# Rebuilding the tail of an encoder layer: the embedding product moved into the last attention units, all tokens through seven-product passes 384 columns wide, weight splits placed later

## The chip, the cores and the metric

The kernel runs on one core of a Trainium2 chip. The metric is device time in microseconds of one execution. Three runs of the kernel before took 2616.91, 2618.83 and 2621.61 us; the median is 2618.83. The engines are called by their short names: PE (TensorE), DVE (VectorE), ACT (ScalarE), POOL (GpSimd) and SP (SyncE, which issues the transfers).

## The reference

Two sequences (a prompt and a sample) of 2048 tokens, model width 1024, share one set of weights; all is float32.

```python
def encoder_layer(x, p, norm_w, w_in, ..., w_out, w_ple, w_ple_gate):
    h = rms_norm(x, norm_w)
    q_a, k_a, v_a, g_a, q_b, k_b, v_b, g_b = jnp.split(h @ w_in, IN_SPLITS, axis=-1)
    ...
    o_a = windowed_gqa_sink(q_a, k_a, v_a, sink_a) * jax.nn.silu(g_a)
    ...
    o_b = neighbourhood_attn(q_b, k_b, v_b, rpb_b) * jax.nn.silu(g_b)
    x = x + jnp.concatenate([o_a, o_b], axis=-1) @ w_out
    gate = jax.nn.sigmoid(x @ w_ple_gate)
    return x + (p @ w_ple) * gate
```

Branch A is attention in a window of 128 tokens to each side (8 query heads, 2 key heads, width 64), with QK-norm, a partial rotary embedding and a sink for each head. Branch B is neighbourhood attention over a grid of 64 columns (8 heads) with QK-norm and a position bias. `p` has 256 columns.

## The kernel before

**Float32 by three passes.** Each operand of a matmul is split into a high part (a rounded `fp32r` copy, made by ACT) and a low part (the rest, a subtraction on DVE or POOL), and each product is three matmuls: hi·hi, lo·hi, hi·lo. In the profile a split of a weight shows as ACT L146 and DVE L147 (`split_w`, with the norm's weight as a factor), or L150 and L151 (without).

**Phases.** Phase A goes over 32 tiles of 128 tokens, with two attention units each (`sc` scores, `pt` transposes, `po` output), phase B over 64 units of 128 tokens and 4 heads (`scb`, `ptb`, `pob`). Between an attention unit's steps the program puts matmuls of a *stream* of other work, which a generator gives out step by step: the projections of phase A (`pk`, `pq`, `pg`), then those of phase B (`pqk`, `pvg`, twice, for two halves of the heads), then `out_ahead`. `PLAN_A` and `PLAN_B` say at which share of a unit's budget of PE time which step comes; the last units have a budget of `TAIL`. Each engine works through its own instructions in the order that results from this. SP issues all transfers in one order.

**Weights.** The weights of the stream lie in 16 slots `wa0..7` and `wb0..7`. When a part of the stream ends, `paired` loads the next weights over them with `load_w`, which also puts one job (a split) for each slot into the list `jobs`. Every fourth step of the stream runs one job (`pump`); at the start of a projection `flush("wa")` or `flush("wb")` runs all of that name that are left. `stats_b` (L512), a few small DVE operations that make the norm's factors for a sequence from its sums of squares, is called when a projection has been given out.

**The tail.** The out projection of the first 4 tiles of 256 tokens is done by `out_ahead` (L811) as a plain product over 1024 rows, 192 matmuls of 256 columns each (`pout`), three tiles inside the last attention units and one behind them; the sum with `x` is made by DVE L831 (`ev`) and written to DRAM (`x_d`). The remaining 6 groups of 512 tokens of the out projection (stage 0) and all 8 of the gate (stage 1) go through a scheme of seven products of half-size blocks in place of eight: the weights' sums are prepared in phase A (`sums`), `prep` makes the seven right operands (`opd`, from the raw blocks `oar`, `obr` or `x1r`; sums on DVE and POOL at L993 to L1004, high part ACT L977/L979, low part DVE or POOL L993), `product` (L1014) issues 48 matmuls 256 columns wide for each, into accumulators `acca` and `accc`, and `result` evacuates them: a copy into `r` by ACT (L1059) or a sum with `x` by DVE (L1054), later sums into `r` (L1064), and in stage 1 a tanh on ACT (L1068), the product with the embedding part (DVE L1069) and the sum with `x1` (DVE L1071). The embedding product `pple` (768 matmuls of 256) stands between the products of stage 1. `prep` runs two products ahead of `product`. Accumulators come in the PSUM pools of the phases before (`pj` three buffers, `sc` three, `ms` two).

Of the kernel before, what the change touches and what calls it, by code (L numbers as in the profile page):

```python
# [18 lines left out]
SEQ = 2048  # L19
# [51 lines left out]
TW = 256  # L71
NU = SEQ // TW
AHEAD = 4
# [15 lines left out]
def emit(ctx, tc, io):  # L89
# [3 lines left out]
    pp = ctx.enter_context(tc.tile_pool(name="psum", bufs=2, space=bass.MemoryType.PSUM))  # L93
# [50 lines left out]
    def split_w(w, raw, sc, pin=lambda ins: ins):  # L144
        if sc is not None:
            nc.scalar.activation(w[:, 0], raw, AF.Copy, scale=sc)  # L146
            nc.vector.scalar_tensor_tensor(out=w[:, 1], in0=raw, scalar=sc, in1=w[:, 0].bitcast(F32),  # L147
                                           op0=ALU.mult, op1=ALU.subtract)
        else:
            pin(nc.scalar.copy(w[:, 0], raw))  # L150
            pin(nc.vector.tensor_tensor(out=w[:, 1], in0=raw, in1=w[:, 0].bitcast(F32), op=ALU.subtract))  # L151

    jobs = []
# [9 lines left out]
    def load_w(pool, tag, src, c0, nk, scaled):  # L163

        ws = []
        for j in range(nk):
# [3 lines left out]
            jobs.append((tag, partial(split_w, w, raw, nw[:, j:j + 1] if scaled else None)))  # L170
# [67 lines left out]

    P = tc.keep_in_program_order
# [144 lines left out]
    def proj_a(f):  # L384
# [41 lines left out]
        for i, c in enumerate(project(pq, xr, lambda k, b: w_q[k][:, b, :], 215)):  # L426
# [6 lines left out]
            if i == PD and late:  # L433
                late.pop()()
            yield c
# [36 lines left out]
        if f == NT + 9:  # L472
            stats_b(0)
# [130 lines left out]
    def proj_b(f):  # L604
# [5 lines left out]
        if f == 2 * NT + 9:  # L610
            stats_b(1)
# [4 lines left out]
        flush("wa")  # L616
        pk = ptile([128, 512], "pj", "pqk")
        for i, c in enumerate(project(pk, xr, lambda k, b: w_qk[k][:, b, :], 215)):
            at = i + 24 if f in last else i
            if at in HX:  # L620
                split(f + 1, HX[at])
            yield c
# [15 lines left out]
        flush("wb")  # L638
        pv = ptile([128, 512], "pj", "pvg")
        for i, c in enumerate(project(pv, xr, lambda k, b: w_vg[k][:, b, :], 215)):  # L640
# [117 lines left out]
    tiles = [(s, u) for s in range(2) for u in range(NU)]  # L758
    x1_d = [dram.tile([128, KT, TW], F32, tag=f"x1_d{n}", name=f"x1_d{n}") for n in range(len(tiles))]
    o_st, o_rs = {}, {}  # L760

    def fproj(ps, w, m, xs, nk, mm_):
        for k in range(nk):
            if mm_ is mm:
                flush(f"o{k // 4}")
                flush(("wa", "wb")[m // 4])
            for i, (a, b) in enumerate(((0, 0), (1, 0), (0, 1))):
                mm_(ps, w[m // 4][k][:, a, 128 * (m % 4):128 * (m % 4) + 128], xs(k, b),
                    start=(k == 0 and i == 0), stop=(k == nk - 1 and i == 2))
                yield 108  # L770

    def load_o(n, tail):
        if n < len(tiles):
            s, u = tiles[n]
            o_st[n] = []
            for i in range(2):
                st = main.tile([128, 2, TW], F32, tag="stage", name="oa", bufs=2)
                nc.sync.dma_start(st, oa_d[s].rearrange("(i j p) t -> i p j t", p=128, j=2)[i, :, :, TW * u:TW * u + TW])
                o_st[n].append(st)
            for i in range(2):  # L780
                if tail:
                    st = ap.tile([128, 2, 4, 64], F32, tag="sq", name="ob", bufs=2)
                else:
                    st = main.tile([128, 2, 4, 64], F32, tag="s", name="ob", bufs=SB)
                nc.sync.dma_start(st.rearrange("p j c t -> p (j c) t"),
                                  ob_d[s][u // 2].rearrange("p (i j) c t -> i p (j c) t", i=2)
                                  [i, :, :, 64 * (u % 2):64 * (u % 2) + 64])
                o_st[n].append(st)

    def split_o(n, i):  # L790

        t = main.tile([128, 2, 2, 2, TW], F32R, tag="xr", name="o_r", bufs=2)
        st = o_st[n][2 * i:2 * i + 2]

        def job(dst, src):
            nc.scalar.copy(dst[0], src)
            nc.vector.tensor_tensor(out=dst[1], in0=src, in1=dst[0].bitcast(F32), op=ALU.subtract)
        for j in range(2):
            if i == 0:
                jobs.append((f"o{i}", partial(job, [t[:, j, a] for a in range(2)], st[j])))  # L800
            else:
                for k in range(2):
                    jobs.append((f"o{i}", partial(job, [t[:, j, a, k].rearrange("p (r k c) -> p k r c", k=4, c=16)
                                                        for a in range(2)],
                                                  st[j][:, k].rearrange("p k (r c) -> p k r c", c=16))))
        o_rs.setdefault(n, []).append(t)

    def o_hi_lo(n):
        return lambda k, b: o_rs[n][k // 4][:, k % 4 // 2, b, k % 2, :]

    def out_ahead(n):  # L811

        tail = n < AHEAD - 1
        if n > 0:
            split_o(n, 0)
            split_o(n, 1)
        if n != AHEAD - 2:
            load_o(n + 1, tail)
# [398 lines left out]
```

## Time and profile before

| | |
|---|---|
| median of three runs | 2618.83 us |
| the profiled execution | 2626.2 us |
| its span in the trace | 2624.4 us |
| granted TensorE clock, mean | 0.99 |
| PE, DVE, ACT, POOL busy | 2552.9, 1959.5, 1416.7, 788.5 us |
| instructions of PE | 16080 matmuls |
| moved by DMA | 357.51 MB, mean 136 GB/s |

A row of the timeline or of the chain gives start and length in us, engine, line of the kernel, operation, output <- inputs and shape; `xN` means that N of the same kind stand in one row. In brackets stands how long the engine had been idle and what released it. A line such as L193 is that of the helper that issues all matmuls, so the names of the tiles tell the place. Granted clock 1.00 is full speed.

### The profile page before, as it was taken

The page shows a single profiled execution, that of the slowest core. Times are in us where ns is not written, and L with a number is a line of the kernel's source. Part 1 is how long each engine was busy: PE and PEld are TensorE (multiplying, and loading weights), DVE is VectorE, ACT ScalarE, POOL GpSimd, SP SyncE. Part 2 cuts the span into 40 slices and gives each one's busy share as a digit, 9 for nine tenths or more (in the row PEclk, how much of TensorE's full clock was granted, in tenths as well). Part 3 has the DMA queues.
Part 4 walks back from the last instruction along what each step waited for, and adds up shares of the span by engine and source line. Part 5 has one row for each costly group of instructions (what it writes and reads, how often), then busy time and mean ns, then how long its engine had stood idle before and what let it go on. Part 6 is the DMA issues. An engine that isn't in the chain of part 4 may idle for free.

```text
span 2624.4 us, 46991 instructions
## 1 busy us (share of the span) xinstructions
PE 2552.9 (97%) x16080; PEld 2274.5 (87%) x16080; DVE 1959.5 (75%) x5702; ACT 1416.7 (54%) x3327; POOL 788.5 (30%) x996
## 2 busy tenths in 40 slices
PE   7999999999979999999899999999999999999999
PEld 6888888888867888888788888887999999999999
DVE  6888888888877788888888888888655548555554
ACT  5666666666655566666666666666432214222322
POOL 3332333322323333333233332221122323223321
PEclk9999999999999999999999999999999999999999
DMA  5333322111133555555755555457575446232221
GB/s 176 107 105 105 107 83 93 57 57 59 57 91 118 160 174 170 183 175 157 241 160 162 188 176 152 151 158 214 177 245 183 150 158 208 81 108 97 78 79 47
DMA packets 227520, 357.51 MB, mean 136 GB/s; under 512 B 37937, under 2 KB 115377, under 8 KB 222129
## 3 DMA queue, kind: packets, MB, share of 16 engines
q1 hardware_dynamic: 227280, 354.50, 42.8%
q8 instruction: 128, 2.10, 0.3%
q14 instruction: 112, 0.91, 0.1%
HBM read 266.33 MB, written 105.92 MB: 142 GB/s over the span
## 4 chain that ended last, share of the span: by engine, by line
PE 87%; DVE 6%; DMA 4%; ACT 2%; issue 1%; POOL 0%; SPq 0%; ACTq 0%; DVEq 0%; POOLq 0%
PE pqk L193 13%; PE pvg L193 13%; PE acca L1027 12%; PE accc L1027 9%; PE pg L193 6%; PE pq L193 5%; PE pob L193 4%; PE pple L193 3%; PE scb L193 3%; PE ptb L196 3%; PE sc L193 3%; PE po L193 3%; PE pt L196 3%; PE pk L193 3%; PE pout L193 3%
## 5 line engine op out<-in xcount | busy, mean ns | idle before, releaser
L223 ACT ACTIVATE s<-s,nm 128x384 f32<-128x384 f32 (+4 forms) x512 | 306.4, 600 | 344.3 <-DVE nm L219 185.5
L193 PE MATMUL pvg<-wb,xr 128*128 128x512 f32 x1536 | 458.9, 406 | 0.0
L193 PE MATMUL pqk<-wa,xr 128*128 128x512 f32 x1536 | 436.6, 406 | 0.0
L288 POOL TENSOR_TENSOR xr<-stx,xr 128x512 fp32r<-128x512 f32 x192 | 248.0, 1299 | 205.9 <-ACT xr L287 203.1
L193 PEld LDWEIGHTS pqk<-wa,xr 128*128 128x128 f32 x1536 | 266.8, 189 | 37.2
L193 PEld LDWEIGHTS pvg<-wb,xr 128*128 128x128 f32 x1536 | 270.0, 190 | 32.1
L193 PE MATMUL pg<-wb,xr 128*128 128x512 f32 x768 | 233.0, 411 | 4.3 <-DVE q L445 4.3
L193 PE MATMUL pq<-wa,xr 128*128 128x512 f32 x768 | 223.3, 404 | 3.3 <-ACT wa L146 3.3
L234 POOL TENSOR_TENSOR g<-qg,rd 128x256 f32<-128x256 f32 x64 | 39.4, 615 | 494.0 <-DVE rd L232 480.1
L1027 PE MATMUL acca<-opd,s 128*128 128x256 f32 x1344 | 164.3, 283 | 2.5 <-ACT r L1059 2.5
L193 PEld LDWEIGHTS pq<-wa,xr 128*128 128x128 f32 x768 | 141.5, 192 | 28.1 <-ACT wa L146 3.7
L1027 PEld LDWEIGHTS acca<-opd,s 128*128 128x128 f32 x1344 | 162.6, 192 | 2.9 <-ACT r L1059 2.7
L208 DVE CUSTOM_DVE_ANT_0 s<-scb,bias 128x288 f32<-128x288 f32 (+3 forms) x256 | 141.9, 555 | 28.8 <-PE scb L193 24.5
L193 PEld LDWEIGHTS pg<-wb,xr 128*128 128x128 f32 x768 | 138.6, 191 | 25.2 <-issue 4.6
L721 ACT CAST p_t<-ptb 96x384 fp32r<-96x384 f32 (+3 forms) x256 | 130.0, 509 | 50.1 <-PE ptb L196 48.5
L722 DVE TENSOR_TENSOR p_t<-ptb,p_t 96x384 fp32r<-96x384 f32 (+3 forms) x256 | 149.0, 584 | 9.0 <-ACT p_t L721 6.3
L600 ACT ACTIVATE ks_b<-pktb,wk 64x128 fp32r<-64x128 f32 x256 | 125.5, 490 | 44.4 <-DVE ks_b L601 38.6
L193 PEld LDWEIGHTS pob<-p_t,vw 128*128 128x128 f32 (+2 forms) x832 | 132.6, 189 | 19.0 <-ACT wa L146 0.6
L601 DVE SCALAR_TENSOR_TENSOR ks_b<-pktb,wk,ks_b 64x128 fp32r<-64x128 f32 x256 | 115.1, 449 | 40.1 <-ACT ks_b L600 33.6
L993 POOL TENSOR_TENSOR opd<-sum,opd 128x1024 fp32r<-128x1024 f32 x28 | 69.6, 2486 | 238.1 <-ACT opd L979 238.1
L193 PE MATMUL sc<-ks_a,q 128*128 128x384 f32 (+1 forms) x512 | 122.6, 339 | 18.9 <-DVE pr L560 13.0
L560 DVE TENSOR_TENSOR pr<-pt,pr 128x512 fp32r<-128x512 f32 x184 | 123.4, 682 | 22.9 <-ACT pr L559 22.4
(197 smaller groups left out, 5941.7 us busy)
## 6 DMA issues: line engine op xcount, KB each, us to landing
stx<-x_b SPq DMA_DIRECT2D x128, 256.0 KB
vw<-v_d SPq DMA_DIRECT2D x112, 256.0 KB
stx<-x_a SPq DMA_DIRECT2D x64, 256.0 KB
stn<-x_n SPq DMA_DIRECT2D x64, 256.0 KB
v_d<-vb SPq DMA_DIRECT2D x64, 256.0 KB
x1r<-x_d SPq DMA_DIRECT2D x16, 1024.0 KB
y_t<-r SPq DMA_DIRECT2D x64, 256.0 KB
v_d<-vb SPq DMA_DIRECT2D x96, 128.0 KB
```

What stands on the lines that cost most here:

```text
L193: pinned(nc.tensor.matmul(out, lhsT, rhs, start=start, stop=stop))
L196: pinned(nc.tensor.transpose(out, in_, ident))
L208: nc.vector.tensor_tensor_reduce(out=s[:, :n], in0=ps[:, :n], in1=bias, scale=1.0, scalar=-3.0e38, op0=ALU.add, op1=ALU.max, accum_out=sm[ ...
L223: nc.scalar.activation(ss[i][:, :n], ss[i][:, :n], AF.Exp, bias=nm[:, i:i + 1], accum_out=den[:, i:i + 1])
L288: nc.gpsimd.tensor_tensor(out=lo, in0=raw, in1=hi.bitcast(F32), op=ALU.subtract)
L560: nc.vector.tensor_tensor(out=pr[:, 1], in0=pf, in1=pr[:, 0].bitcast(F32), op=ALU.subtract)
L600: nc.scalar.activation(hi, pkt[a:a + 64, i], AF.Copy, scale=wk[a:a + 64, 1:2])
L601: nc.vector.scalar_tensor_tensor(out=lo, in0=pkt[a:a + 64, i], scalar=wk[a:a + 64, 1:2], in1=hi.bitcast(F32), op0=ALU.mult, op1=ALU.subtract)
L721: nc.scalar.copy(p_t[:kc, :nch, 0], pf)
L722: nc.vector.tensor_tensor(out=p_t[:kc, :nch, 1], in0=pf, in1=p_t[:kc, :nch, 0].bitcast(F32), op=ALU.subtract)
L993: each(lambda x, y, z: eng.tensor_tensor(out=x, in0=y, in1=z, op=ALU.subtract), out, a, b)
L1027: pinned(nc.tensor.matmul(ps[:, kk], w[k][:, a, c:c + 128], o[:, b, k], start=i in (0, 1, 4) and kk == 0 and k == 0 and j == 0, stop=k == ...
```

## The change

What moves, in words:

- `out_ahead` is gone. All 4096 tokens of both stages go through the seven products. A group is now the same rows of both sequences (`ROWS`: 4, 6, 6, 6, 6, 4 rows of 64 tokens, so 256 or 384 columns of each sequence); the two columns of blocks are the two sequences. 12 groups of 336 matmuls, 2688 of them 384 wide and 1344 of them 256 wide.
- The embedding product becomes `ple_ahead`: 12 tiles of 48 matmuls (192 of 256 columns, 384 of 384), nine inside the last attention units, three behind them. Its results are halved on the way out of PSUM, by ACT and DVE in turn, and written to DRAM (`ple_d`); stage 1 reads them back, with `x1`, as `ins` (two loads for each result, three buffers).
- The accumulators are eight tiles of a new PSUM pool, `a0..a3` and `c0..c3`, with one buffer each, opened once `pple` is done. Tanh, the product with the embedding part and the sum before them work in PSUM in place.
- Raw blocks are loaded one by one into five buffers (at products 2, 4 and 5); the high and low parts of an operand are tiles of their own. The blocks of branch B are loaded in pieces of 128, 256 or 384 bytes.
- `load_w` and `load_q` put splits into `jobs` with a name for each slot. After a load, `HOLD` steps of the stream pass before the first split, then every second step runs one; `ready` runs those that are left just before the matmuls that use the slot. Splits keep the program's order (`P`).
- `stats_b` is called in the middle of a projection.
- Slots of the tail: the embedding weights in `wa0..3`, the quarters `a12` in `wa4..7`, `a11` and `a22` in `wb`, later `s4` in `wa0..3`.

```diff
+HOLD = {"wa": 20, "wb": 12, "s2": 60}
+ROWS = (4, 6, 6, 6, 6, 4)
...
+GT = tuple(64 * r for r in ROWS)
...
+    def ready(tag, k, w):
+        flush(f"{tag}{k + 1}")
+        flush(f"{tag}{k}")
+        return w[k]
...
+        hold[0] = HOLD[tag[:2]]
...
-            jobs.append((tag, partial(split_w, w, raw, nw[:, j:j + 1] if scaled else None)))
+            jobs.append((f"{tag}{j}", partial(split_w, w, raw, nw[:, j:j + 1], P)))
...
+            if i == PD + 1 and f == NT + 9:
+                stats_b(0)
...
-        flush("wa")
         pk = ptile([128, 512], "pj", "pqk")
-        for i, c in enumerate(project(pk, xr, lambda k, b: w_qk[k][:, b, :], 215)):
+        for i, c in enumerate(project(pk, xr, lambda k, b: ready("wa", k, w_qk)[:, b, :], 215)):
...
+    def split_p(n, k):
...
+            P(nc.scalar.copy(hi, src))
+            P(nc.vector.tensor_tensor(out=lo, in0=src, in1=hi.bitcast(F32), op=ALU.subtract))
...
+    def ple_ahead(n):
+        g, s = divmod(n, 2)
+        nt = GT[g]
+        load_p(n + 1)
+        flush("wp")
+        for m in range(KT):
+            ps = ptile([128, 512], "pj", "pple")[:, :nt]
+            for k in range(2):
+                w = w_p[m // 4, k]
+                for i, (a, b) in enumerate(((0, 0), (1, 0), (0, 1))):
+                    mm(ps, w[:, a, 128 * (m % 4):128 * (m % 4) + 128], p_rs[n][:, b, k, :nt],
+                       start=(k == 0 and i == 0), stop=(k == 1 and i == 2))
+                    yield MMC[nt]
...
+            if m % 2:
+                nc.vector.tensor_scalar_mul(ev, ps, 0.5)
+            else:
+                nc.scalar.activation(ev, ps, AF.Copy, scale=0.5)
+            nc.sync.dma_start(ple_d[g][s][:, m], ev)
...
-            elif n % 4 == 3:
+            elif hold[0] > 0:
+                hold[0] -= 1
+            elif n % 2:
                 pump()
...
+                t = op.tile([128, 4 * GMAX], F32, tag="raw", name="raw", bufs=5)[:, :4 * nt]
...
+            for mq in range(4):
                 if i in (0, 1, 4):
-                    acc[key, mp] = ptile([128, 2, TW], "pj" if key == "a" else "sc", "acc" + key)
+                    acc[key, mq] = pt.tile([128, 512], F32, tag=f"{key}{mq}", name="acc" + key, bufs=1)[:, :GT[g]]
...
+            t = ins[key] = main.tile([128, 2, 512], F32, tag="p_t", name="ins", bufs=3)[:, :, :GT[g]]
...
+                nc.sync.dma_start(t[:, 0], ple_d[g][s][:, m])
+                nc.sync.dma_start(t[:, 1], x1_d[g][s][:, m])
...
+            v = r if q == (1, 1) else ps
             if q != (0, 1):
+                V.tensor_tensor(out=v, in0=ps, in1=r, op=ALU.add)
+            nc.scalar.activation(v, v, AF.Tanh, scale=0.5)
+            V.scalar_tensor_tensor(out=v, in0=v, scalar=1.0, in1=t[:, 0], op0=ALU.add, op1=ALU.mult)
+            V.tensor_tensor(out=r, in0=v, in1=t[:, 1], op=ALU.add)
+            load_in()
...
+                elif i == 12 and n == 2 * NG - 1:
+                    prep(0)
+                elif i == 36 and n == 2 * NG - 1:
+                    prep(1)
+        pp_stack.close()
+        pt = ctx.enter_context(tc.tile_pool(name="psum2", bufs=1, space=bass.MemoryType.PSUM))
```

ACT at the end of phase A, where the weights `wa` of phase B are split (`s` are the exponentials of an attention unit, `ot` its output, `pr` its transposed probabilities; the number behind `wa` tells the slots apart). Before:

```order
L579 COPY ot<-po 64x256 x2
L245 CAST q_10040<-pqt 64x512
L146 ACTIVATE wa_10115<-wa_10115,nw 128x512
L411 ACTIVATE vv<-pk,y 128x2x64
L146 ACTIVATE wa_10117<-wa_10117,nw 128x512
L245 CAST q_10041<-pqt 64x512
L559 CAST pr<-pt 128x512 x2
L146 ACTIVATE wa_10119<-wa_10119,nw 128x512
L559 CAST pr<-pt 128x512
```

Now:

```order
L257 CAST q_10049<-pqt 64x512
L237 ACTIVATE s,den<-s,nm 128x384 x4
L242 ACTIVATE es<-es 128x4
L591 COPY ot<-po 64x256 x2
L152 ACTIVATE wa_10123<-wa_10123,nw 128x512
L473 ACTIVATE gs<-pg,y 128x512
L152 ACTIVATE wa_10125<-wa_10125,nw 128x512
L571 CAST pr<-pt 128x512
L299 CAST xr<-stx 128x512
```

The first split stood ahead of the second `q` cast of a unit; it now stands behind that cast, the unit's exponentials and its `ot`, and other work lies between the splits.

DVE at the start of the seven-product loop (`s_...` are weight sums being split, `opd` or `lo` low parts of operands, `sum` operand sums, `ev` evacuations of `pout` or `pple`). Before:

```order
L151 TENSOR_TENSOR s_24977<-s_24977 128x512
L151 TENSOR_TENSOR s_24979<-s_24979 128x512
L993 TENSOR_TENSOR opd<-oar,opd 128x1024
L993 TENSOR_TENSOR opd<-obr,opd 128x256 x4
L996 TENSOR_TENSOR sum<-sum,oar 128x1024
L831 TENSOR_TENSOR ev<-pout,ev 128x512 x2
L1054 TENSOR_TENSOR r<-acca,xres 128x512 x2
L993 TENSOR_TENSOR opd<-sum,opd 128x1024
```

Now:

```order
L818 TENSOR_TENSOR p_r<-p_25176,p_r 128x256
L157 TENSOR_TENSOR s_25089<-s_25089 128x512
L997 TENSOR_TENSOR lo<-raw,hi 128x256 x4
L1000 TENSOR_TENSOR sum<-sum,raw 128x4x256
L843 TENSOR_SCALAR ev<-pple 128x256 x6
L1066 TENSOR_TENSOR r<-acca,ins 128x256 x4
L997 TENSOR_TENSOR lo<-sum,hi 128x4x256
```

In both, an operand sum of the third product stands ahead of the last evacuations; there are now six of `pple` behind it where there were two of `pout`, and the splits of `s` lie apart.

412 lines of the change are left out of this document (181 added, 231 removed).

## The prediction

> **What bounds the kernel now.** I read the page first (busy shares, then the chain of work that ended last), then busy time by windows, then the timeline at each window in which TensorE is not full.
>
> ```profile
> span 2624.4 us, 46991 instructions
> PE 2552.9 (97%) x16080; PEld 2274.5 (87%) x16080; DVE 1959.5 (75%) x5702; ACT 1416.7 (54%) x3327; POOL 788.5 (30%) x996
> PE 87%; DVE 6%; DMA 4%; ACT 2%; issue 1%; POOL 0%; SPq 0%; ACTq 0%; DVEq 0%; POOLq 0%
> ```
>
> TensorE is busy for 97% and is 87% of the chain. So there are two currencies only: columns that TensorE no longer multiplies, and stretches in which it stands or runs at a lower granted clock. All other work is free as long as it stays beside TensorE. Windows show the second currency (columns: window, length, then busy us of PE, PEld, DVE, ACT, POOL, then granted clock, DMA share, GB/s):
>
> ```profile
> 600.00:620.00 20.00, 17.51 (x99) 14.96 (x99) 17.92 (x73) 10.57 (x28) 5.93 (x9) 0.97 0.20 66
> 740.00:760.00 20.00, 11.51 (x50) 9.86 (x51) 12.04 (x39) 12.08 (x27) 1.56 (x2) 0.74 0.32 94
> 1280.00:1300.00 20.00, 18.41 (x85) 15.23 (x85) 16.38 (x35) 13.74 (x29) 4.73 (x6) 0.83 0.75 230
> 1820.00:1840.00 20.00, 19.74 (x149) 19.06 (x148) 16.63 (x36) 11.10 (x25) 2.16 (x4) 0.91 0.69 199
> 1940.00:1960.00 20.00, 14.63 (x83) 14.07 (x83) 12.45 (x14) 5.21 (x10) 11.01 (x10) 0.75 0.73 261
> 2220.00:2240.00 20.00, 17.49 (x146) 17.29 (x145) 16.11 (x20) 10.23 (x17) 6.03 (x2) 1.00 0.12 41
> 2240.00:2600.00 360.00, 360.00 (x3002) 360.00 (x3002) 188.65 (x228) 105.08 (x147) 102.78 (x46) 1.00 0.26 84
> ```
>
> The last row is the seven-product loop in steady state: no TensorE time lost in 360 us, DVE at 52%. The others are the places where the program changes phase. A shortfall of the clock by 0.26 over 20 us is worth 5.2 us, by 0.09 1.8 us.
>
> **Columns.** What one matmul costs, from starts of neighbouring rows:
>
> ```profile
> 42.14 3.47 PE L193 MATMUL pg<-wb,xr 128*128 128x512 f32 x14
> 45.45 0.60 PE L196 MATMUL pqt<-ident,q 128*128 128x128 f32 x4
> 75.78 0.86 PE L193 MATMUL sc<-ks_a,q 128*128 128x384 f32 x4
> 76.48 0.39 PE L193 MATMUL pq<-wa,xr 128*128 128x512 f32 x1
> 2581.74 11.52 PE acca L1027 x96
> ```
>
> 512 columns: (45.45 − 42.14)/14 = 0.236 us. 256 columns: 11.52/96 = 0.120. Halfway, 384 columns should take 0.178; the one short run of 384 gives (76.48 − 75.78)/4 = 0.175. I take 0.178. The tail before is 4 × 192 `pout` + 14 × 336 products + 768 `pple` = 6240 matmuls of 256, 748.8 us. After: 192 + 1344 = 1536 of 256 (184.3 us) and 384 + 2688 = 3072 of 384 (546.8 us), 731.1 us. **Term 1: −17.7 us.** Of it 24,576 columns, which the 1024 tokens of `pout` save with seven products in place of eight, are 11.5 us at 0.120 per 256; the rest is fewer, wider matmuls. The bounds are −11.5 (a column costs the same at any width) and −26.9 (0.175).
>
> The Trainium skill, page "TensorE: Matmul & The Clock Gate", section "Wait — 56ns, not 53.3ns?", has N/2.4 GHz plus 2.5 ns for a warm matmul, 109 ns at 256 columns and 216 at 512; the rows are 10% above it, so the rows decide. By its figures, as an estimate, the term would be −14.5 us.
>
> **A to B (around 745 us).** Weights of phase B go over the slots of phase A.
>
> ```profile
> 736.28 0.62 PE L193 MATMUL pg<-wb,xr 128*128 128x512 f32 x2
> 748.50 0.98 PE L193 MATMUL sc<-ks_a,q 128*128 128x384 f32 x2 [11.59 <-DVE pr L560]
> 745.69 0.72 ACT L146 ACTIVATE wa<-wa,nw 128x512 fp32r<-128x512 f32 x1 [12.12 <-DMA wa<-w_in_c]
> 756.78 0.75 ACT L579 COPY ot<-po 64x256 f32<-64x256 f32 x2
> 768.10 0.73 ACT L146 ACTIVATE wb<-wb,nw 128x512 fp32r<-128x512 f32 x1 [4.28 <-DMA wb<-w_in_c]
> 768.85 0.39 PE L193 MATMUL pqk<-wa,xr 128*128 128x512 f32 x1
> ```
>
> ACT stands 12.12 us at a split of `wa` whose load has not landed. Behind it in ACT's order is a `q` cast, then the `pr` casts; DVE and TensorE wait for those. The weight itself is wanted only by the first `pqk`, 20 us later. In the new order the first split stands behind the unit's exponentials and its `ot` copies, which ACT did at 756.78; 11.59 earlier that is 745.2, about when the load lands. So the 11.59 go, and of the 5.2 at half clock most. `wb` may stop ACT as the 4.28 did, now closer to the first `pqk`; I keep 3 us back for that. **Term 2: −14**, bounds −5 (wait halved, clock kept) and −17.
>
> The Trainium skill, same page, section "What's actually happening", has a free-running window of 3.4 us and half clock after an idle one. The 0.74 above agrees, some three such windows. By it a remaining wait of 3 us could still cost one window, 1.7 us, and the term would be −12.
>
> **Statistics, and the boundaries inside phase B.**
>
> ```profile
> 618.12 0.62 PE L193 MATMUL sc<-ks_a,q 128*128 128x384 f32 x2 [2.46 <-DVE mx L208]
> 1281.59 0.76 PE L193 MATMUL scb<-ks_b,q1b 128*128 128x512 f32 x1 [3.65 <-DVE mx L208]
> 1303.46 0.47 PE L193 MATMUL scb<-ks_b,q1b 128*128 128x512 f32 x1 [1.53 <-DVE vrb L629]
> 1819.63 0.51 PE L193 MATMUL pout<-o_r,wa 128*128 128x256 f32 x2 [2.62 <-DVE o_r L797]
> ```
>
> `stats_b` is a chain of small DVE operations in program order, now issued in the middle of a projection rather than at its end, when scores wait for DVE. 2.46 and half of the 3.4 around it at half clock: **term 3: −4**, bounds 0 (the chain only delays another score) and −5.
> Around 1280 the same 16 splits must still be done, but one each second step and not ahead of `scb`. Idle of 3.65 + 1.53 and 3.4 us of clock (0.17 × 20), of which I take under half: **term 4: −4**, bounds +2 and −8. DVE is at 82% there, so the work has little room.
> At 1819 the splits of `o_r` go, but `p_r` casts take their place for the first `pple`: **term 5: −1**, bounds +3 and −4.
>
> **Into the seven-product loop (around 1950).**
>
> ```profile
> 1944.57 0.47 PE L1027 MATMUL acca<-opd,wa 128*128 128x256 f32 x2 [0.87 <-issue]
> 1953.94 2.26 PE L1027 MATMUL acca<-opd,wa 128*128 128x256 f32 x9 [3.76 <-DVE ev L831]
> 1986.08 1.19 PE L1027 MATMUL accc<-opd,wb 128*128 128x256 f32 x8 [3.17 <-ACT opd L979]
> ```
>
> Before, 12 splits of `s` came in one block, then an operand sum that waits for POOL, and the last `ev` behind that. After, splits come apart by `pump` and by step, and two operands are made within the last `pple`; but six `ev` of `pple` still stand behind a sum that waits for POOL. 7.8 us idle and 5 us of clock (0.25 × 20): **term 6: −4**, a third, bounds +5 and −12.
> The stage switch:
>
> ```profile
> 2224.37 1.81 PE L1027 MATMUL acca<-opd,s 128*128 128x256 f32 x13 [2.51 <-ACT r L1059]
> ```
>
> The same work meets there: 0, bounds −2 and +3.
>
> **Inside the loop** nothing was lost before; does it stay so with single accumulators, with one evacuation per 384 columns, and with `pple` read back from DRAM?
>
> ```profile
> L1071 DVE SCALAR_TENSOR_TENSOR r<-r,x1r 128x512 f32<-128x512 f32 x56 | 46.1, 823 | 1.7
> L1069 DVE SCALAR_TENSOR_TENSOR r<-r,pple 128x512 f32<-128x512 f32 x56 | 38.4, 686 | 43.9 <-ACT r L1068 43.9
> L1064 DVE TENSOR_TENSOR r<-accc,r 128x512 f32<-128x512 f32 x41 | 28.3, 691 | 35.3 <-PE accc L1027 35.3
> L993 DVE TENSOR_TENSOR opd<-x1r,opd 128x1024 fp32r<-128x1024 f32 x21 | 25.7, 1226 | 36.3 <-ACT opd L979 36.3
> ```
>
> At 384 columns these are three quarters (0.62, 0.51, 0.52 us) and the operand one and a half (1.84). A product with a final result of four quarters costs DVE 4 × 1.65 + 1.84 = 8.4 us against 48 × 0.178 = 8.5 of TensorE: tight for two products in seven, while products without final results are light. A quarter's accumulator is next written three quarters (6.4 us) later at the earliest, which absorbs that. Loads: a group of stage 1 moves 16 × 2 × 0.197 MB of `ins`, 3.1 of raw and 3.1 of results, 12.6 MB in 59.8 us, 211 GB/s; 261 were moved at 1940. SP issues 52 of them, at the 0.32 us of an issue row below 17 of the 59.8 us. **Term 7: 0**, bounds 0 and +10.
>
> **Sum:** −17.7 − 14 − 4 − 4 − 1 − 4 = −44.7 against the profiled execution of 2626.2 us (span 2624.4 and 1.8 around it): 2581.5. The median of the runs shown is 2618.83, 7.4 below; less 44.7 it is **2574 us**.
>
> **Rivals.**
> *The stalls come back elsewhere.* For: the splits, casts and evacuations are as many, and DVE is at 90% in 600:620 and 83% in 1820:1840. Against: the loss at 745 is a wait for a load, not work. Terms 3 to 6 at 0 and half of term 2: −17.7 − 7 + 1 = −24, 2595.
> *The wait at 745 is not removed* (the later split still meets an unlanded load, or the first `pqk` does): without term 2, 2588. For: loads and stores are issued in the same order as before. Against: the 20 us to the first `pqk`.
> *More goes than I take:* all terms at their lower bounds are −74.9, 2544; half way there is −59.8, 2559. For: wide spacing of the splits may empty the boundaries. Against: each needs its own reason to come true.
> *Slower: `ins` cannot keep up.* Three buffers, filled from one queue, in which raw loads and stores stand too; DVE works in order, so a late `ins` stops the operands too.
>
> ```profile
> 758.98 0.32 SPq L169 DMA_DIRECT2D wb<-w_in_c  x1
> 761.98 0.73 ACT L146 ACTIVATE wb<-wb,nw 128x512 fp32r<-128x512 f32 x1 [0.91 <-DMA wb<-w_in_c]
> ```
>
> 256 KB took 3.0 us from issue to use. With 0.4 for a second issue and 1.4 for DVE's two operations and handovers, three results turn in 4.8 us; TensorE makes three in 6.4. If a round trip takes 8.6 us, the turn is 10: four turns of 10 less 25.6, less the 6.4 of slack, cost 8 us in each of six groups, 48 in all, which eats the gain; that is the point of decision. At 9.4 (the crowded load kept ACT for 12.12 at 745) it is 11.2 × 6 = 67 us, 2641. Against: the largest transfer in the loop is 0.8 MB, 3 us at 261 GB/s.
> That the change does not do what it says I exclude: the order of instructions shows it.
>
> **Chances.** Forecast (2562 to 2588) 0.57; stalls elsewhere 0.17; the wait stays 0.08; more goes 0.10; `ins` cannot keep up 0.08, of which 0.03 near the point of decision. Range 2550 to 2600: it leaves out the `ins` case, a few hundredths of the first rival and of "more goes". A measurement tells about 0.2%, 5 us, from no change: faster 0.92, same 0.03, slower 0.05.
>
> **What would show it.** Step by step: no idle of TensorE above 3 us near 736, and a clock near 1.0 there; `pple` and products of 384 at 0.178 from start to start; at most 12 us lost between the last score and the third product; windows inside stage 1 with PE at 100%, DVE near 70%. It is wrong if TensorE's waits inside the loop name `ins`, DVE's `r`, or an operand in each group, or if a 384-wide matmul takes over 0.18.

## The result and the profile after

The changed kernel took 2657.17 us (median of 4 runs, 2653.68 to 2662.8) beside 2619.32 for the kernel before: a ratio of 1.0147, 95% interval 1.0124 to 1.017. It is 1.5% slower; 2574 was forecast, and the range ended at 2600.

The page after, busy shares and chain:

```profile
span 2651.7 us, 44703 instructions
PE 2538.8 (96%) x14448; PEld 2250.7 (85%) x14448; DVE 2035.9 (77%) x5868; ACT 1450.2 (55%) x3413; POOL 782.2 (29%) x970
PE 71%; DVE 9%; DMA 9%; issue 5%; ACT 4%; POOL 2%; SPq 1%; DVEq 0%; POOLq 0%; ACTq 0%
```

TensorE is still busy for 96%, but it is only 71% of the chain that ended last, 87% before. DVE, DMA and the issue of work have taken its place. Windows of the changed kernel (PE, PEld, DVE, ACT, POOL busy, then clock, DMA share, GB/s), first at the three boundaries of the projections, then through the tail:

```profile
600.00:620.00 20.00, 19.89 (x113) 17.14 (x112) 17.54 (x67) 12.52 (x36) 5.90 (x9) 1.00 0.18 60
740.00:760.00 20.00, 18.28 (x96) 14.68 (x95) 19.00 (x36) 16.87 (x36) 7.25 (x7) 1.00 0.67 206
1280.00:1300.00 20.00, 17.95 (x99) 14.59 (x98) 18.11 (x53) 12.83 (x29) 5.98 (x7) 1.00 0.51 163
...
1780.00:1940.00 160.00, 133.21 (x766) 121.02 (x765) 97.18 (x228) 82.17 (x197) 17.04 (x27) 0.93 0.58 185
1940.00:2020.00 80.00, 61.80 (x446) 60.63 (x445) 49.49 (x78) 24.08 (x47) 20.95 (x16) 0.87 0.74 210
2020.00:2280.00 260.00, 255.65 (x1529) 254.77 (x1528) 145.44 (x209) 49.10 (x60) 81.04 (x50) 1.00 0.55 163
2280.00:2360.00 80.00, 69.71 (x515) 69.16 (x515) 66.66 (x102) 35.21 (x67) 27.54 (x9) 0.89 0.72 227
2360.00:2651.00 291.00, 272.78 (x1662) 269.57 (x1660) 192.50 (x262) 104.54 (x171) 67.93 (x21) 0.99 0.60 188
```

The first two rows are what was hoped for: at 740 TensorE is busy for 18.28 of 20 us (11.51 before) at full clock, at 600 for 19.89. At 1280 the clock is full (0.83 before), but TensorE is busy for less than it was there (17.95 us against 18.41). From 1780 on it is the reverse: 27 us without a matmul in the last attention units, 18 around the start of the new loop, 10 at the change of stage and, from 2360 to the last matmul, 11.5 in stage 1, whose steady state had none before.

Where the difference sits is told by three places that both programs have. The rows are from the timeline of the changed kernel, TensorE's alone (start and length in us): the first matmul of phase B's projections (`pqk`), the first of the tail's work, and the first of the products:

```profile
750.82 0.39 PE L207 MATMUL pqk<-wa,xr 128*128 128x512 f32 x1
1791.01 0.48 PE L207 MATMUL pple<-p_r,wp 128*128 128x256 f32 x2
1974.90 0.48 PE L1029 MATMUL acca<-hi,a 128*128 128x256 f32 x2 [1.65 <-ACT ev L845]
```

The first `pqk` was at 768.85 before, so 18.0 us are won up to there. The tail's first matmul in the timeline of the kernel before, whose first product begins at 1944.57:

```profile
1813.44 0.48 PE L193 MATMUL pout<-o_r,wa 128*128 128x256 f32 x2
```

| stretch, us | before | after | difference |
|---|---|---|---|
| start to the first matmul of the tail's work | 1813.4 | 1791.0 | −22.4 |
| from there to the first product (*fill*) | 131.1 | 183.9 | +52.8 |
| first product to the last matmul (*loop*) | 674.6 | 669.4 | −5.2 |
| behind the last matmul | 5.2 | 7.4 | +2.2 |

The sum is +27.4, the difference of the two spans in the traces. The medians differ by 37.9: the profiled execution of the kernel before (2626.2 us) was longer than all four timed runs, and that of the changed kernel (2653.68) was its shortest, so the traces show the lower end of the loss. And a product of 384 columns is cheaper than reckoned. The chain in a quiet stretch of stage 0:

```profile
2072.37 16.64 PE acca L1029 x96
```

16.64/96 = 0.1733 us for 384 columns. So the tail's matmuls take 1536 × 0.120 + 3072 × 0.1733 = 716.7 us in place of 748.8: 32.1 saved, of which 29.5 in the loop and 2.6 in the fill. The loop holds 627.1 us of matmuls after and 656.6 before, so it lost 42.3 us where it had lost 18; the fill lost 55.4 us more than before. Of these 55.4, TensorE standing still makes 35.7 (40.4 us against 4.7); the granted clock, 0.89 on average in the fill against 0.99, accounts for most of the rest (an estimate: 0.11 × 183.9 less 0.01 × 131.1, 19 us).

**What TensorE waited for in the fill** (waits of the changed kernel from 1780 to 2020: us, times, longest):

```profile
PE pple L207 <- DVE ev L843: 17.1, 11, 7.6
PE pple L207 <- ACT ev L845: 15.7, 13, 4.0
PE pple L207 <- ACT p_r L817: 5.4, 1, 5.4
```

For evacuations, then. What ACT and DVE waited for ahead of those (waits of the changed kernel, 1780 to 1980):

```profile
ACT ev L845 <- DMA ple_d<-ev: 31.1, 21, 2.9
DVE ev L843 <- DMA ple_d<-ev: 20.1, 15, 4.8
```

Two pieces of its chain in that stretch, from issue to landing (start and length in us):

```profile
1845.59 6.83 DMA ple_d<-ev
1861.26 5.12 DMA ple_d<-ev
```

An evacuation needs a buffer `ev`; there are two, and each is held until its write to DRAM has landed (is complete), 6.8 and 5.1 us after its issue in these pieces, the longest. Nine more pieces of the chain in the attention units, also writes that something waited for, last 1.9 to 4.2 us from issue to landing; the eleven average 3.6. 72 results come in the 150 us of the attention units, one each 2.1 us, so a buffer has 4.2 us for its turn. The evacuation itself takes 0.5 of them, so by this average two buffers leave next to nothing over, and a landing that takes longer stops an engine. ACT and DVE work in order, so the attention's own casts stand behind the waiting evacuation too.

**In stage 1** a group looks like this on POOL, DVE and TensorE of the changed kernel:

```profile
2451.14 6.98 POOL L997 TENSOR_TENSOR sum<-raw 128x1536 f32<-128x1536 f32 x2 [10.86 <-DMA raw<-x_d]
...
2454.69 5.05 DVE L1000 TENSOR_TENSOR sum<-sum,raw 128x1536 f32<-128x1536 f32 x1 [7.52 <-POOL sum L997]
...
2461.93 0.62 PE L1029 MATMUL accc<-hi,a 128*128 128x384 f32 x2 [1.71 <-DVE r L1083]
```

A raw block lands late, POOL makes two subtractions one right behind the other, DVE stands 7.52 us for the first and then, beside the second, needs 5.05 for an addition of 1536 columns, where its subtractions of that size take 1.75 (L997 `lo<-raw,hi`, 16 of them in 27.9 us), and the results behind it are late for TensorE. At the end of each group DVE waits again, several times, for the read-back (waits of DVE from 2280 on, then what TensorE waited for there):

```profile
DVE lo L997 <- ACT hi L982: 36.9, 11, 8.0
DVE sum L1000 <- POOL sum L997: 28.7, 5, 7.5
DVE acca L1085 <- DMA ins<-ple_d: 21.3, 18, 3.2
```

```profile
PE acca L1029 <- DVE r L1086: 9.4, 7, 3.2
PE accc L1029 <- DVE r L1083: 8.0, 4, 4.5
```

TensorE waits for DVE's `r`, a sign of being wrong that the prediction had named. The longest wait of DVE, for ACT's casts `hi`, is not the cause: it is longer still (57.3 us) in e3_raw_once below, where TensorE stands for less.

### The profile page after: what moved, and what is told of

Same layout as the page of the kernel before. It is cut to its first block, busy times and chain, and to the rows that moved or that the text cites. A ratio compares the mean times of both kernels' runs of the same rounds, so it can differ in the third digit from the quotient of the medians.

```text
span 2651.7 us, 44703 instructions
## 1 busy us (share of the span) xinstructions
PE 2538.8 (96%) x14448; PEld 2250.7 (85%) x14448; DVE 2035.9 (77%) x5868; ACT 1450.2 (55%) x3413; POOL 782.2 (29%) x970
## 4 chain that ended last, share of the span: by engine, by line
PE 71%; DVE 9%; DMA 9%; issue 5%; ACT 4%; POOL 2%; SPq 1%; DVEq 0%; POOLq 0%; ACTq 0%
PE pqk L207 12%; PE pvg L207 12%; PE acca L1029 7%; PE pg L207 6%; PE pq L207 5%; PE accc L1029 4%; PE pob L207 3%; PE scb L207 3%; PE ptb L210 3%; PE pt L210 3%; PE pk L207 3%; PE po L207 3%; PE sc L207 3%; DMA ple_d<-ev 2%; DMA ins<-ple_d 2%
## 5 line engine op out<-in xcount | busy, mean ns | idle before, releaser
L1029 PE MATMUL acca<-hi,s 128*128 128x384 f32 (+1 forms) x1152 | 265.6, 318 | 0.9 <-DVE r L1066 0.9
L1029 PEld LDWEIGHTS acca<-hi,s 128*128 128x128 f32 x1152 | 199.8, 190 | 1.2 <-issue 1.1
L1029 PE MATMUL accc<-hi,a 128*128 128x384 f32 (+1 forms) x768 | 179.4, 321 | 14.8 <-DVE r L1083 8.0
L1029 PE MATMUL acca<-lo,s 128*128 128x384 f32 (+1 forms) x576 | 183.0, 318 | 0.0
L997 POOL TENSOR_TENSOR lo<-sum,hi 128x1536 fp32r<-128x1536 f32 (+1 forms) x24 | 76.8, 3200 | 345.6 <-ACT hi L982 335.4
L207 PE MATMUL pple<-p_r,wp 128*128 128x384 f32 (+1 forms) x576 | 126.1, 355 | 38.7 <-DVE ev L843 17.1
L982 ACT CAST hi<-sum 128x1536 fp32r<-128x1536 f32 (+1 forms) x48 | 64.2, 1338 | 180.5 <-PE acca L1029 98.7
L997 POOL TENSOR_TENSOR sum<-raw 128x384 f32<-128x384 f32 (+3 forms) x72 | 120.7, 1705 | 141.8 <-DMA raw<-x_d 55.3
```

The lines of the kernel that those rows point to most:

```text
L207: pinned(nc.tensor.matmul(out, lhsT, rhs, start=start, stop=stop))
L982: fn(*views)
L997: each(lambda x, y, z: eng.tensor_tensor(out=x, in0=y, in1=z, op=ALU.subtract), out, a, b)
L1029: pinned(nc.tensor.matmul(ps, w[k][:, a, 128 * mq:128 * mq + 128], o[b][:, k], start=i in (0, 1, 4) and k == 0 and j == 0, stop=k == 3 and ...
```

## The experiments

Two theories for the fill: E, the two evacuation buffers; and its rival, that the writes and SP's single order are too slow whatever the buffers. Three for the loop: R, raw blocks come late because five buffers hold a group and a quarter; I, the read-back `ins`; and S, which came up during the experiments, the operand sums on POOL. Ratios are to the kernel before, run beside each; fill and loop are from each kernel's trace.

| kernel | median us | ratio (95%) | fill | loop |
|---|---|---|---|---|
| before | 2619 to 2623 | 1 | 131.1 | 674.6 |
| changed | 2657.17 | 1.0147 (1.0124 to 1.017) | 183.9 | 669.4 |
| e1_front | 2605.61 | 0.9934 (0.9918 to 0.9951) | 132.9 | 676.5 |
| e2_ev5 | 2635.40 | 1.0053 (1.0033 to 1.0073) | 159.1 | 676.8 |
| e3_raw_once | 2640.07 | 1.0071 (1.0045 to 1.0096) | 180.7 | 654.9 |
| e4_no_ple | 2636.31 | 1.0056 (1.0036 to 1.0076) | 183.7 | 657.8 |
| e5_pin | 2628.81 | 1.0028 (1.0014 to 1.0043) | 156.2 | 672.3 |
| e6_w256_raw8 | 2668.20 | 1.0176 (1.0147 to 1.0206) | 166.7 | 699.7 |
| e7_w256_raw5 | 2699.62 | 1.0296 (1.0266 to 1.0326) | 168.9 | 729.4 |
| e8_w256_pairs | 2667.02 | 1.0172 (1.0142 to 1.0202) | 166.8 | 701.3 |
| e9_front_pin | 2603.24 | 0.9936 (0.992 to 0.9953) | 131.6 | 672.1 |
| e10_pr_early | 2624.17 | 1.0013 (1.0003 to 1.0023) | 154.2 | 670.3 |
| e11_sums_dve | 2596.66 | 0.9908 (0.9889 to 0.9928) | 154.6 | 640.7 |
| e12_sums_only | 2621.71 | 0.9992 (0.998 to 1.0004) | 178.8 | 642.2 |
| e13_second_sum | 2637.63 | 1.0053 (1.0033 to 1.0073) | 184.0 | 653.9 |

**e1_front.** The kernel before with the change's first part alone.

```diff
+        hold[0] = HOLD[tag] if scaled else 0
...
+                jobs.append((f"{tag}{j}", partial(split_w, w, raw, nw[:, j:j + 1], P)))
...
-        flush("wa")
-        for i, c in enumerate(project(pk, xr, lambda k, b: w_qk[k][:, b, :], 215)):
+        for i, c in enumerate(project(pk, xr, lambda k, b: ready("wa", k, w_qk)[:, b, :], 215)):
```

> The kernel before with only the first part of the change: weight splits of phase B held, one by one and just in time (HOLD, ready, every second step), and the statistics in the middle of a projection; the tail as before. If terms 2, 3 and 4 were right and the loss is all in the tail: 16 to 22 us faster than before, about 2599. If the early part only looks better because the tail pays for it (splits or loads pushed later): within 6 us of before.

Measured: 2605.61, 17 us below the 2622.47 beside it. The old tail starts at 1791.2, as the new one does, and its fill and loop are within 2 us of those of before. The first part of the change is sound, and all of the loss is in the tail.

**e2_ev5.**

```diff
-            ev = (ap.tile([128, 512], F32, tag="ev", name="ev", bufs=2) if n < AHEAD else
+            ev = (ap.tile([128, GMAX], F32, tag="ev", name="ev", bufs=5) if n < AHEAD else
```

> The changed kernel with five buffers of 384 columns in place of two of 512 for the evacuated embedding product inside the attention units. Theory: each buffer is held until its write to DRAM has landed, some 5.5 us against one new tile each 2.1 us, so two buffers stall ACT, DVE and then TensorE; with five the loss between 1797 and 1940 us shrinks by 15 to 25 us, time about 2636. Rival (the writes themselves or SP's order are too slow, buffers only shift the wait): under 6 us gained.

Measured: 2635.40, 22 us less; the fill shrinks by 24.8. The waits of ACT and DVE in it (1780 to 1980 of e2_ev5):

```profile
ACT ev L845 <- DMA ple_d<-ev: 7.2, 2, 3.6
...
DVE ev L843 <- DMA ple_d<-ev: 9.2, 2, 5.3
```

31.1 + 20.1 have become 7.2 + 9.2. Theory E holds; its rival falls as the main cause, since the writes are as many and in the same order. In this trace the loop is 7.4 us longer than in the changed kernel's; why, no run shows.

**e3_raw_once and e4_no_ple**, the changed kernel with part of stage 1's loads left out in turn: the raw blocks of four of its six groups, then the half of the read-back that comes from `ple_d`. Neither computes the layer.

```diff
+            if stage == 1 and g > 1:
+                for h, s in which:
+                    raws[n, h, s] = raws[n - 1, h, s][:, :, :nt]
+                return
```

> The changed kernel, but stage 1 loads the raw blocks only for its first two groups and uses the second group's blocks for the later ones, so no raw load waits for a buffer there (the loads of four groups are left out, and their outputs are not the layer's). Theory R (five raw buffers hold one group and a quarter, so a raw block comes late, POOL's operand sum waits for it, DVE stands behind that sum and TensorE behind DVE): stage 1 after its first group loses under 4 us in place of about 15 over 2340 to 2651; total 2642 or less. Theory I (the loss there is the read-back): gain under 4 us.

```diff
-                nc.sync.dma_start(t[:, 0], ple_d[g][s][:, m])
...
-            V.scalar_tensor_tensor(out=v, in0=v, scalar=1.0, in1=t[:, 0], op0=ALU.add, op1=ALU.mult)
+            V.scalar_tensor_tensor(out=v, in0=v, scalar=1.0, in1=t[:, 1], op0=ALU.add, op1=ALU.mult)
```

> The changed kernel, but stage 1 reads back only x1 and uses it in place of the embedding product as well (half of the read-back loads are left out; the output is not the layer's). Theory I (three buffers for the read-back, each filled by two loads behind others in SP's order, hold DVE up): stage 1 gains 8 to 15 us, total about 2645. Theory R: under 4 us.

Measured: 2640.07 and 2636.31, 17 and 21 us less; the loop loses 14.5 and 11.6 less. Each theory had said that the other's experiment gains under 4. Both were wrong in that: either one takes about half of the 24.3 us away that the loop lost more than before. DVE's waits from 2270 on, of e3_raw_once and then of e4_no_ple:

```profile
DVE acca L1089 <- DMA ins<-ple_d: 18.7, 18, 2.6
...
DVE sum L1004 <- POOL sum L1001: 11.9, 5, 2.9
```

```profile
DVE sum L1000 <- POOL sum L997: 23.6, 5, 6.2
...
DVE acca L1084 <- DMA ins<-x_d: 9.7, 9, 2.1
```

In the first the wait for the read-back is nearly as long as it was (18.7 of 21.3), in the second the wait for POOL (23.6 of 28.7), and yet from 2360 on TensorE hardly stands in either. Windows from there to the last matmul: changed kernel, e3_raw_once, e4_no_ple, and e12_sums_only from further below:

```profile
2360.00:2644.30 284.30, 272.75 (x1662) 269.57 (x1660) 189.95 (x257) 104.17 (x170) 67.93 (x21) 1.00 0.60 189
2360.00:2625.90 265.90, 265.90 (x1638) 265.74 (x1636) 178.38 (x256) 104.33 (x168) 73.70 (x21) 1.00 0.50 158
2360.00:2630.50 270.50, 268.76 (x1652) 268.12 (x1650) 189.54 (x258) 103.88 (x169) 68.76 (x22) 1.00 0.47 146
2360.00:2611.30 251.30, 249.48 (x1540) 248.63 (x1538) 181.86 (x252) 96.97 (x158) 25.83 (x8) 1.00 0.63 199
```

It stands for 11.5 us in the changed kernel, for 0, 1.7 and 1.8 in the others. A quarter's accumulator leaves 36 matmuls, 6.2 us, of slack; the reading that fits all three is that one of the two waits fits into it and both in a group do not. (Before 2360, in the first groups, e3_raw_once still loses one piece of 7.5 us, so theory R's own figure, under 4 us in stage 1 behind its first group, was missed.) And where no raw block is loaded, POOL's two subtractions no longer follow one another, and the addition is as short as any (e3_raw_once):

```profile
2437.59 1.76 DVE L1004 TENSOR_TENSOR sum<-sum,raw 128x1536 f32<-128x1536 f32 x1 [2.93 <-POOL sum L1001]
```

**e5_pin**, on top of e2_ev5: the last evacuations stay ahead of the third product's operand sum. In the changed kernel DVE had it the other way round, with TensorE behind it:

```profile
1960.92 3.34 DVE L1000 TENSOR_TENSOR sum<-sum,raw 128x1024 f32<-128x1024 f32 x1 [1.30 <-POOL sum L997]
...
1964.75 8.51 PE L207 MATMUL pple<-p_r,wp 128*128 128x256 f32 x48 [7.64 <-DVE ev L843]
```

```diff
-                nc.vector.tensor_scalar_mul(ev, ps, 0.5)
+                pin(nc.vector.tensor_scalar_mul(ev, ps, 0.5))
...
-                V.tensor_tensor(out=src, in0=src, in1=b11, op=ALU.add)
+                (P if m == 2 else lambda ins: ins)(V.tensor_tensor(out=src, in0=src, in1=b11, op=ALU.add))
```

> e2_ev5, and the last evacuations of the embedding product keep their place in program order ahead of the operand sum of the third product (on DVE and ACT), which waits for POOL and for loads. If that order costs TensorE its 7.64 us before the last tiles: 5 to 9 us faster than e2_ev5, about 2628. If the loads behind it are the bound: within 3 us of e2_ev5, the wait moves to the first products.

Measured: 2628.81, 6.6 us below e2_ev5, inside what was expected for the order, though the two intervals overlap and the fill is only 2.9 us shorter. TensorE's wait for DVE there was 8.00 us in e2_ev5; in e5_pin it is 5.22, and what DVE then waits for is the landing of a write:

```profile
1937.21 0.42 DVE L844 TENSOR_SCALAR ev<-pple 128x256 f32<-128x256 f32 x1 [3.28 <-DMA ple_d<-ev]
...
1937.68 7.50 PE L207 MATMUL pple<-p_r,wp 128*128 128x256 f32 x48 [5.22 <-DVE ev L844]
```

So the order is worth some 3 us of this wait. The rest is a ring of buffers again: the last three tiles evacuate into the five buffers of `s`, which e2_ev5 does not touch.

**e7_w256_raw5, e6_w256_raw8, e8_w256_pairs**: 256 columns throughout (with seven buffers `ev`), then eight raw buffers, then the read-back in pairs.

```diff
-ROWS = (4, 6, 6, 6, 6, 4)
+ROWS = (4,) * 8
-AHEAD = 9
+AHEAD = 12
...
-            ev = (ap.tile([128, 512], F32, tag="ev", name="ev", bufs=2) if n < AHEAD else
+            ev = (ap.tile([128, GMAX], F32, tag="ev", name="ev", bufs=7) if n < AHEAD else
...
-                t = op.tile([128, 4 * GMAX], F32, tag="raw", name="raw", bufs=5)[:, :4 * nt]
+                t = op.tile([128, 4 * GMAX], F32, tag="raw", name="raw", bufs=8)[:, :4 * nt]
...
-                nc.sync.dma_start(t[:, 0], ple_d[g][s][:, m])
+                nc.sync.dma_start(t[:, 0], ple_d[g][s][:, m:m + 2])
```

> The changed kernel 256 columns wide throughout (eight groups of four rows, 16 embedding tiles, 12 of them inside the attention units), seven evacuation buffers, five raw buffers as in the change. It is the base of the next two. TensorE's own work rises by 6 us against 384 wide; raw blocks are two thirds as large and groups two thirds as long, so the waits in stage 1 stay if five buffers are the cause: about 2640.

> e7_w256_raw5 with eight raw buffers, which hold two groups, in place of five. Theory R (late raw blocks): 8 to 15 us faster than e7_w256_raw5. Theory I alone (the read-back): under 4 us.

> e6_w256_raw8 with the read-back loaded for two results at a time, so the same three buffers hold six results and half as many loads are issued. Theory I: 5 to 12 us faster than e6_w256_raw8. If the raw blocks were all: within 3 us. DVE alone as bound (smaller operations at 256 columns): no change.

Measured: 2699.62, 2668.20 and 2667.02. The base is 60 us slower than expected. Some 14 of them are a slip of the expectation, which reckoned 6 us more work for TensorE: 3072 matmuls of 0.1733 us become 4608 of 0.120, about 20 us more. For the other 46 the narrow form has a trouble of its own. Eight raw buffers take 31.4 off it: late raw blocks matter, more than R had said. Pairs bring 1.2, nothing. In e8_w256_pairs DVE waits for something else again (2270 to 2650):

```profile
DVE r L1088 <- DMA y_t<-r: 42.8, 15, 5.5
```

The eight buffers of the results are now the ring that waits for its stores to land. Whether that alone makes the narrow form slow was not tried.

**e9_front_pin.** The lesson of e5_pin put on e1_front.

```diff
-            nc.vector.tensor_tensor(out=ev, in0=ps, in1=ev, op=ALU.add)
+            (P if not tail else lambda ins: ins)(nc.vector.tensor_tensor(out=ev, in0=ps, in1=ev, op=ALU.add))
...
-                V.tensor_tensor(out=src, in0=src, in1=b11, op=ALU.add)
+                (P if m == 2 else lambda ins: ins)(V.tensor_tensor(out=src, in0=src, in1=b11, op=ALU.add))
...
-            sub(G if i in (2, 4) else V, lo, src, hi.bitcast(F32))
+            if m == 1:
+                each(lambda x, y, z: P(V.tensor_tensor(out=x, in0=y, in1=z, op=ALU.subtract)), lo, src, hi.bitcast(F32))
+            else:
+                sub(G if i in (2, 4) else V, lo, src, hi.bitcast(F32))
```

> e1_front (old tail, new first part), and the last two evacuations of the out projection keep their place ahead of the operand sum of the third product on DVE. The lesson of e5_pin carried to the old tail: the 3.76 us before the first product go, 3 to 5 us faster than e1_front (ratio to before about 0.992). If the wait there is for the loads of raw blocks: no change against e1_front.

Measured: 2603.24, ratio 0.9936 against 0.9934: no gain that can be told, though in the traces the fill is 1.3 us and the loop 4.4 us shorter. The wait for `ev` falls from 4.73 us in e1_front to 1.47, and waits of 0.8 to 2.3 us for `r` stand behind it instead. A miss.

**e10_pr_early**, on top of e5_pin. The changed kernel's first `pple` waits for a cast that could be made earlier:

```profile
1797.55 0.80 PE L207 MATMUL pple<-p_r,wp 128*128 128x256 f32 x2 [5.45 <-ACT p_r L817]
```

```diff
             split_p(0, 0)
+            split_p(0, 1)
         yield from b
...
-            split_p(0, 1)
```

> e5_pin, and the second half of the first embedding operand is split with the first half instead of after the last projection, so the first product of the embedding does not wait 5.45 us for ACT's cast. Theory: 5 to 8 us faster than e5_pin, about 2622. Rival: the matmul then waits for the next thing (weight splits), under 2 us.

Measured: 2624.17, 4.6 less, just under the 5 to 8 of the theory, and the fill is 2 us shorter. The two intervals overlap, so whether it helps at all isn't clear of the noise. The trace shows why it is so little: the wait of 5.4 us for the cast is gone, but waits of 1.7 and 2.4 us for DVE's `qg` have come in its place, much as the rival had it.

**e11_sums_dve**, on top of e10_pr_early, then **e12_sums_only** and **e13_second_sum** on the changed kernel itself.

```diff
             if i == 2:
-                sub(G, src, b22, b12)
+                sub(V, src, b22, b12)
...
             elif i == 3:
-                sub(G, src, b12, b11)
+                sub(V, src, b12, b11)
             elif i == 4:
-                sub(G, src, b22, b12)
+                sub(V, src, b22, b12)
```

(e13_second_sum has the one at `i == 3` alone.)

> e10_pr_early with all operand sums of the seven products on DVE (three per group move from POOL, 1.75 us each at 384 columns), so DVE no longer stands behind POOL's subtraction. If the in-order wait for POOL (28.7 us in stage 1 of the changed kernel) is what makes the late results: 8 to 15 us faster than e10_pr_early. If the raw blocks themselves are late, DVE waits for them instead: within 4 us. If DVE is too full: slower.

> The changed kernel with nothing else altered than that all operand sums of the seven products are made by DVE (three subtractions per group leave POOL). If the 27 us of e11_sums_dve are this edit's own: 22 to 30 us faster than the changed kernel (2657), about 2630. If they needed the freed evacuation and order first: under 15 us.

> The changed kernel with only the fourth product's subtraction moved from POOL to DVE; the third's stays on POOL, so DVE still waits for one subtraction. If DVE's addition takes 4 to 5 us in place of 1.75 because POOL's second subtraction runs beside it, the addition falls to about 1.8 us and most of the gain of e12_sums_only comes already here (over 10 us). If the wait for the first subtraction is the cost: under 5 us.

Measured: 2596.66, 27.5 below e10_pr_early; 2621.71, 35 below the changed kernel; 2637.63, 19.5 below it. The loop falls to 640.7, 642.2 and 653.9. e11_sums_dve and e12_sums_only gained more than any theory had said. DVE's addition in the changed kernel, in e13_second_sum and in e12_sums_only (count, us in all, ns of one, idle before):

```profile
L1000 DVE TENSOR_TENSOR sum<-sum,raw 128x1536 f32<-128x1536 f32 x8 | 37.1, 4633 | 33.7 <-POOL sum L997 33.7
```

```profile
L1000 DVE TENSOR_TENSOR sum<-sum,raw 128x1536 f32<-128x1536 f32 x8 | 14.0, 1752 | 13.7 <-POOL sum L997 13.7
```

```profile
L1000 DVE TENSOR_TENSOR sum<-sum,raw 128x1536 f32<-128x1536 f32 x8 | 14.0, 1752 | 0.0
```

The mean of 4633 ns hides two sizes: seven of the eight additions take 5.04 or 5.05 us beside POOL's second subtraction, and the eighth, beside none, 1.74. In the group shown further above, POOL's second subtraction ran on for 3.4 us after the addition had begun, and the addition took 3.3 us more than alone. Without that subtraction beside it the addition takes 1.75 us. The wait for POOL falls from 33.7 to 13.7, but not all of this is won, since DVE now waits for a raw block itself. A group of e13_second_sum:

```profile
2442.22 1.76 DVE L997 TENSOR_TENSOR sum<-raw 128x1536 f32<-128x1536 f32 x1 [3.86 <-DMA raw<-x_d]
2442.28 5.06 POOL L997 TENSOR_TENSOR sum<-raw 128x1536 f32<-128x1536 f32 x1 [10.47 <-DMA raw<-x_d]
2447.38 1.76 DVE L1000 TENSOR_TENSOR sum<-sum,raw 128x1536 f32<-128x1536 f32 x1 [3.40 <-POOL sum L997]
```

Here it is POOL, beginning second, that needs 5.06 us where its subtractions of that size take 3.5 in the changed kernel. About half of the loop's gain (15.5 of 27.2) comes with the short addition and the shorter wait together. The rest comes when DVE need not wait for POOL at all. The Trainium skill, page "SBUF — State Buffer", section "Who interferes with whom", says that a DVE instruction with two inputs in SBUF contends with a GpSimd instruction that reads SBUF; 5.05 against 1.74 us agrees. DVE itself was not too full: it is busy for 207.5 of 280 us in stage 1 of e11_sums_dve.

```profile
2300.00:2580.00 280.00, 273.78 (x1662) 272.45 (x1662) 207.51 (x279) 107.54 (x174) 32.83 (x10) 0.99 0.63 197
```

e11_sums_dve beats both kernels: 2596.66, ratio 0.9908, all of the change with four corrections to its tail. But e1_front, with the old tail, has 0.9934, and the two intervals overlap: what the corrected tail adds to the first part, some 7 us by these ratios, is not clear of the noise. Its fill is still 154.6 us. TensorE stands for 22.8 of them (4.7 before) at a clock of 0.93 (0.99 before), and most of that at two places, near the last tiles:

```profile
1924.75 6.43 PE L207 MATMUL pple<-p_r,wp 128*128 128x256 f32 x30 [7.00 <-ACT ev L846]
...
1934.92 0.38 ACT L846 ACTIVATE ev<-pple 128x256 f32<-128x256 f32 x1 [5.97 <-DMA ple_d<-ev]
...
1936.64 7.86 PE L207 MATMUL pple<-p_r,wp 128*128 128x256 f32 x48 [5.47 <-DVE ev L844]
```

ACT and DVE wait there for writes out of the ring `s`. No run gave that ring more buffers, so this last part is read from the trace and not shown.

## Why the prediction was wrong

- **A to B, statistics, first boundary of phase B (terms 2, 3, 4: −14, −4, −4).** Right in size and place: terms 2 and 3 said −18, and the first `pqk` comes 18.0 us earlier; −22 was said for all three, the tail's work starts 22.4 us earlier, and e1_front shows that it holds by itself.
- **Columns (term 1: −17.7).** Mis-sized in the kernel's favour: 384 columns take 0.1733 us, not the 0.178 half way between 256 and 512, so −32.1. The interpolation went wrong at its upper end: 0.236 for 512 columns came from a single row. Nine others in the kernel before take (1015.42 − 1013.35)/9 = 0.230, and half way from there to 0.120 is 0.175, which the short run of four had shown too. The estimate that stands beside this term comes to −14.3 by its own figures, not −14.5.

```profile
1013.35 2.23 PE L193 MATMUL pqk<-wa,xr 128*128 128x512 f32 x9
1015.42 0.40 PE L193 MATMUL scb<-ks_b,q1b 128*128 128x512 f32 x1
```

- **From the last attention units into the loop (terms 5 and 6: −1, −4).** Here the prediction failed most. The step "terms 5 and 6" counted which casts and splits move, and term 1 counted the matmuls of `pple`, but no term held the 96 evacuations with their writes to `ple_d`, nor asked how long a buffer stays taken. With two buffers, a result each 2.1 us and landings of 1.9 to 6.8 us, the fill lost 55.4 us more; e2_ev5 gives 24.8 of it back, e5_pin and e10_pr_early 2.9 and 2. About 26 stay, in e11_sums_dve too. Its trace shows waits for the ring `s` and a lower clock there; no run took them away, so for these 26 us the cause stays open.
- **Six `ev` behind a sum that waits for POOL.** Seen and named, priced at nothing more than before; TensorE stood 7.64 us there. e5_pin shows that the order is a part of it only, some 3 us; the rest of the wait is for a buffer.
- **Inside the loop (term 7: 0).** The loads in GB/s, DVE's 8.4 against 8.5 us and the slack of 6.4 were reckoned each alone. Missing were the late raw blocks, which push POOL's two subtractions together, the addition that takes 5.05 beside POOL in place of the 1.84 reckoned for an operand, and the fact that a second wait in the same group, for `ins`, uses the same slack. The loop lost 24 us more than before; with the sums on DVE (e12_sums_only) it is 27 shorter.
- **The rivals.** "Slower: `ins` cannot keep up" had the right place and sign at 0.08, and DVE does wait for `ins`, 3.2 us at the longest. No view gives the round trip that was to decide at 8.6. That this alone made the kernel slower is not what the runs show: in e12_sums_only the wait is nearly as long (18.8 us of 21.3) and TensorE hardly stands. "The stalls come back elsewhere" was right in the word only: it priced gains that fail to come, and those of terms 2 to 4 came in full. What came on top were new stalls in the tail, 55.4 and 24.3 us more than before, where that rival had reckoned 21.

## What to carry to other kernels

Where a result leaves through a small ring of buffers to DRAM, compare the number of buffers with the landing time in that very stage, here 1.9 to 6.8 us with a result each 2.1: with two buffers and with five the same bytes moved, and the kernel with five was 22 us faster. On an engine that works in order, waits that each fit into the slack of a stage add up: take one away and the others seem free. Before work is spread to a second engine, look whether the first then stands behind it, and whether the two slow each other.

## What the runs showed of the hardware

- A DVE `tensor_tensor` on 1536 columns with both inputs in SBUF took 1.74 to 1.76 us alone and 5.05 when it began beside a POOL subtraction of that size already running; the POOL subtraction took 3.5 us alone and 5.06 when DVE's had begun first (e13_second_sum).
- At full clock a matmul 384 columns wide follows the one before after 0.1733 us, 256 wide after 0.120 and 512 wide after 0.230: 0.451, 0.469 and 0.449 ns for a column, so here only the narrow one costs more for a column.
